# A pooled mix as three products of high and low parts in a decoder layer

## The chip, the core and the metric

The kernel runs on one core of a Trainium2 chip. TensorE multiplies matrices, VectorE and ScalarE do elementwise work and move data out of PSUM, GpSimd (POOL) does some elementwise work too, and SyncE (SP) issues most loads. Each engine takes its instructions strictly in the order in which they were written; where an instruction needs another engine's result it waits on a semaphore, and all behind it on its engine wait too. The metric is the time of one launch on the device, in microseconds (us): the median of three runs.

## The reference

One decoder layer for 256 tokens of width 1024, in float32. The columns of `w_in` give u (512 wide, for the pooling heads) and q, k, v (512 each, for 8 attention heads).

```python
def multiscale_pool(u, w_pool, pool_scale):
    # four groups of 128 channels, windows 2, 4, 8, 16:
    # mean of the trailing window minus the token itself
        groups.append((c_hi - c_lo) / count - uf[..., sl])
    pooled = jnp.stack(groups, axis=2)
    mixed = jnp.einsum('bsgc,gcd->bsgd', pooled, w_pool.astype(jnp.float32))
    return (mixed.reshape(B_, S_, POOL_WIDTH) * pool_scale).astype(u.dtype)

    # the layer
        z = h @ w_in[l]
        pool_out = multiscale_pool(u, w_pool[l], pool_scale[l])
        attn_out = moba_attention(q, k, v).reshape(B_, S_, ATTN_WIDTH)
        mix = jnp.concatenate([pool_out, attn_out], axis=-1) @ w_out[l]
        h = layer_norm(DEEPNORM_ALPHA * h + mix, ln1_g[l], ln1_b[l])
        h = layer_norm(DEEPNORM_ALPHA * h + memory_cross_attention(h, mem, ...), ...)
        h = layer_norm(DEEPNORM_ALPHA * h + swiglu(h, w_gate[l], w_up[l], w_down[l]), ...)
```

With 256 tokens there is one attention block, so the attention is plain causal attention.

## The kernel before

**Products in parts.** Nearly all large products are made of float32 operands that are split in two: a high part, rounded to the type float32r, and a low part, the rest. `split(h, l, ps)` casts on ScalarE (line 483, h) and subtracts on VectorE (line 484, l). `three` (lines 416 to 418) multiplies high by high, high by low and low by high into one accumulator. `proj_both` (lines 431 and 437) has the same three products with the two parts of the activations side by side. A few small products are plain float32: the scores and outputs of the first attention, the transposes, and the four pooled mixes (line 684), which the change touches.

**Weights.** The class `Stream` loads the weights in pieces of 128x1024 (w19, w20, ...), casts each to its high part on ScalarE (line 184, w19h) and subtracts on VectorE (line 191, w19l), some eight pieces ahead of TensorE. A piece that is split frees a raw buffer, and SyncE loads the next piece into it.

**The stretch around the change** (about 50 to 85 us) is written out by hand between the projections of u (`do_u`, accumulators pu) and of the memory's keys (`do_xk`, four chunks of two weight pieces each, accumulators pxk). `run(xk, 8)` lets TensorE do eight steps of that projection, and other work is put between such steps. The four accumulator banks of `accbank` go round: chunk 0 of u, chunk 1 of u, then chunk 0 of the keys (w19, w20) in the banks of the first, chunk 1 (w21, w22) in those of the second. So the first two products with w21h wait until the last two adds of line 704 have read the banks of u's chunk 1.

**The pooling.** u comes out transposed, channels on partitions: a copy on ScalarE (703) and an add on VectorE (704) write it to `upad`. `windows(c)` adds shifted copies on GpSimd (673) for the two groups of a chunk, and scales the first 16 tokens (676). `pool_diff(g)` makes window mean minus token on VectorE (680), in place in `upad`. `mix_pool(g)` multiplies (684); the result, times the scale per channel, is split in cTh (ScalarE, 685) and cTl (VectorE, 686). Groups 0 and 1 belong to chunk 0 of u, groups 2 and 3 to chunk 1. "Mix" one to four below are g = 0 to 3.

`pool_w` holds the four 128x128 mixing matrices and the scales; it is loaded early by one DMA. Activations live in a pool of 11 buffers of 128x2048 floats (tag `a8`), handed out in turn as they come free.

Of the kernel before, what the change touches and what calls it, by code (L numbers as in the profile page):

```python
# [9 lines left out]
F32R = mybir.dt.float32r  # L10
# [4 lines left out]
P = 128  # L15
D = 1024
S = 256
# [9 lines left out]
PADW = 16  # L27
# [14 lines left out]
ALL = slice(None)  # L42
# [4 lines left out]
def r32(t):  # L47
    return t.bitcast(F32)
# [177 lines left out]
def decoder_layer(  # L226
# [3 lines left out]
    nc = tc.nc  # L230
# [3 lines left out]
    ap = ctx.enter_context(tc.tile_pool(name="acts", bufs=A8_BUFS))  # L234
# [10 lines left out]
    def bank(name):  # L245
        return pb.tile([P, 512], F32, tag="b", name=name)
# [59 lines left out]
    class Both:  # L306
# [9 lines left out]
        def pair(self, k, ts=ALL):  # L316
            t, j = self.tiles[k // 4], k % 4
            return t[:, j, 0, ts], t[:, j, 1, ts]
# [29 lines left out]
    pool_w = ep.tile([P, 4 * P + 4], F32, name="pool_w")  # L348
# [59 lines left out]
    upad = ep.tile([P, 4, PADW + S], F32, name="upad")  # L408
# [4 lines left out]
    def three(ps, w, y, start, stop, part=False):  # L413

        (wa, wb), (ya, yb) = w, y
        nc.tensor.matmul(ps, wa, ya, start=start, stop=False, skip_group_check=part)  # L416
        nc.tensor.matmul(ps, wa, yb, start=False, stop=False, skip_group_check=part)  # L417
        nc.tensor.matmul(ps, wb, ya, start=False, stop=stop, skip_group_check=part)  # L418
# [63 lines left out]
    def split(h, l, ps):  # L482
        nc.scalar.copy(h, ps)  # L483
        nc.vector.tensor_sub(l, ps, r32(h))  # L484
# [129 lines left out]
    def scores(hq, t):  # L614
        w = (t + 1) * P
        pss = [bank(f"ps{j}").rearrange("p (h s) -> p h s", h=2) for j in range(2)]
        for h in range(2):
            for j in range(2):
                hs = slice(j * HD, (j + 1) * HD)
                hp = 2 * hq + h  # L620
                nc.tensor.matmul(pss[j][:, h, :w], qT[hs, hp, t * P:(t + 1) * P], kT[hs, hp, :w],
                                 start=True, stop=True)
        todo = []
        for j in range(2):
            pr = sp.tile([P, 2, S], F32, name="pr", bufs=PR_BUFS)[:, :, :w]
            mx = sp.tile([P, 2], F32, name="mx", bufs=6)
            for h in range(2):
                nc.vector.tensor_tensor_reduce(pr[:, h, :], pss[j][:, h, :w], tri[:, S - w:], -1.0, -NEG,  # L628
                                               op0=OP.add, op1=OP.min, accum_out=mx[:, h:h + 1])
            todo.append((pr, exps(pr, pr, mx, -1.0)))  # L630
            probs[hq, t, j] = pr
        for pr, sm in todo:
            scaled(pr, sm)
# [20 lines left out]
    def attend(hp):  # L654
        s0, s1 = pts[hp]
        po = bank("po")
        for j in range(2):
            hs = slice(j * HD, (j + 1) * HD)
            vs = slice((2 * hp + j) * HD, (2 * hp + j + 1) * HD)
            nc.tensor.matmul(po[hs, :S], vt[:, 0, vs], s0[:, j, :], start=True, stop=False)  # L660
            nc.tensor.matmul(po[hs, P:S], vt[:, 1, vs], s1[:, j, :], start=False, stop=True)
        split(cT[0][:, 4 + hp, :], cT[1][:, 4 + hp, :], po[:, :S])
# [4 lines left out]
    def windows(c):  # L667

        cur, n = upad[:, 2 * c:2 * c + 2, :], 1
        for j, g in enumerate((2 * c, 2 * c + 1)):  # L670
# [4 lines left out]
            sums[g] = cur[:, j, :]  # L675
            nc.gpsimd.tensor_mul(sums[g][:, PADW:2 * PADW], sums[g][:, PADW:2 * PADW], fac[:, g, :])

    def pool_diff(g):
        pl = upad[:, g, PADW:]
        nc.vector.scalar_tensor_tensor(pl, sums[g][:, PADW:], 1.0 / WINDOWS[g], pl, op0=OP.mult, op1=OP.subtract)  # L680

    def mix_pool(g):
        pm = bank("pm")
        nc.tensor.matmul(pm[:, :S], pool_w[:, g * P:(g + 1) * P], upad[:, g, PADW:], start=True, stop=True)
        nc.scalar.activation(cT[0][:, g, :], pm[:, :S], AF.Copy, bias=0.0, scale=psc[:, g:g + 1])
        nc.vector.scalar_tensor_tensor(cT[1][:, g, :], pm[:, :S], psc[:, g:g + 1],
                                       r32(cT[0][:, g, :]), op0=OP.mult, op1=OP.subtract)
# [52 lines left out]
    attend(0)  # L740
    scores(1, 1)
    attend(1)
    pool_diff(0)
    pool_diff(1)
    run(u)
    run(xk, 7)
    ws.held = True
    run(xk, 5)
    probs_t(2)
    mix_pool(0)  # L750
    ws.held = False
    run(xk, 8)
    probs_t(3)
    mix_pool(1)
    pool_diff(2)
    run(xk, 8)
    pool_diff(3)
    ws.pace = 2
    run(xk, 8)
    attend(2)  # L760
    attend(3)
    mix_pool(2)
    mix_pool(3)
    run(xk)
# [530 lines left out]
```

## Time and profile before

| | us |
|---|---|
| median of 3 runs (least, most) | 374.09 (374.03, 374.33) |
| the profiled execution | 374.62 |
| its span, first to last instruction | 372.8 |
| TensorE busy (modelled) | 366.7 |
| VectorE busy | 303.1 |
| ScalarE busy | 208.1 |
| GpSimd busy | 24.4 |
| mean granted TensorE clock | 0.999 |

The profiled execution takes 1.8 us more than its span; what lies around the span is the launch. TensorE's busy time is modelled: each product is given a start and an end, and ends overlap the next starts, so the distance of two starts is what a product costs in a row of them. Busy times of VectorE and ScalarE overlap in the same way by about 0.1 us for each instruction.

### The profile page before, as it was taken

What the parts mean: (1) busy time and instruction counts of PE and PEld (TensorE: products, weight loads), DVE (VectorE), ACT (ScalarE), POOL (GpSimd) and SP (SyncE); (2) the same over time, 40 slices, a digit from 0 to 9 for tenths busy, and PEclk for the clock granted to TensorE, in tenths of its full rate; (3) what the DMA queues carried; (4) which work ended last, traced back from release to release, by engine and by line L of the source; (5) the groups of instructions that cost most, each with busy time, mean ns of one, the idle gap of its engine ahead of it and who ended that gap; (6) DMA issues with size and microseconds to landing.
All of it is one profiled execution on the core that took longest, in us unless ns stands there. A gap on an engine that the chain in (4) does not pass through costs nothing.

```text
span 372.8 us, 5508 instructions
## 1 busy us (share of the span) xinstructions
PE 366.7 (98%) x1998; PEld 315.2 (85%) x1998; DVE 303.1 (81%) x493; ACT 208.1 (56%) x336; POOL 24.4 (7%) x31
## 2 busy tenths in 40 slices
PE   9999999999999999999999999999999999999994
PEld 8887878888888889988888888888888888888882
DVE  6878899956699677865889569888888899999994
ACT  5767668635164636644147356766655567774610
POOL 1000033400010000000112000000000000000012
PEclk9999999999999999999999999999999999999999
DMA  7995784658508963688449999955556464896302
GB/s 265 414 416 231 249 310 147 199 173 287 218 2 310 372 220 113 245 289 285 142 65 310 278 303 332 349 180 182 180 194 199 141 225 134 283 355 246 113 0 113
DMA packets 25818, 84.50 MB, mean 227 GB/s; under 512 B 2624, under 2 KB 3392, under 8 KB 25664
## 3 DMA queue, kind: packets, MB, share of 16 engines
q1 hardware_dynamic: 24528, 78.98, 60.2%
q0 software_dynamic: 832, 4.72, 6.4%
q10 hardware_dynamic: 432, 0.46, 0.4%
q8 instruction: 15, 0.25, 0.3%
q14 instruction: 11, 0.09, 0.1%
HBM read 83.10 MB, written 10.49 MB: 251 GB/s over the span
## 4 chain that ended last, share of the span: by engine, by line
PE 98%; ACT 0%; DVE 0%; POOLq 0%; issue 0%
PE pg L431 20%; PE pg L437 10%; PE m L417 5%; PE m L418 5%; PE m L416 5%; PE acc L416 4%; PE acc L417 4%; PE acc L418 4%; PE pxq L431 4%; PE pxk L431 4%; PE pqk L532 4%; PE pqk L535 2%; PE pxk L437 2%; PE pxq L437 2%; PE pu L431 2%; PE xv L416 2%
## 5 line engine op out<-in xcount | busy, mean ns | idle before, releaser
L801 POOL TENSOR_TENSOR rs<-rs,mhalf 128x1 f32<-128x1 f32 x6 | 5.0, 831 | 256.5 <-DVE rs L800 256.5
L483 ACT CAST g<-sg 128x512 fp32r<-128x512 f32 x16 | 9.9, 621 | 21.1 <-DVE sg L1059 13.5
L484 DVE TENSOR_TENSOR g<-sg,g 128x512 fp32r<-128x512 f32 x16 | 11.1, 692 | 11.0 <-ACT g L483 11.0
L1040 DVE TENSOR_TENSOR sg<-pg,sg 128x256 f32<-128x256 f32 x40 | 14.1, 415 | 0.3 <-ACT sg L1039 0.3
L1044 ACT ACTIVATE sg<-sg 128x512 f32<-128x512 f32 x10 | 6.4, 636 | 11.7 <-DVE sg L1040 11.7
L1039 ACT COPY sg<-pg 128x256 f32<-128x256 f32 x40 | 11.8, 376 | 1.3 <-PE pg L437 1.3
L597 ACT ACTIVATE xpr<-xs,mx 128x256 f32<-128x256 f32 x8 | 3.7, 469 | 14.3 <-DVE mx L608 14.3
L597 ACT ACTIVATE pr<-pr,mx 128x128 f32<-128x128 f32 (+1 forms) x16 | 7.1, 445 | 8.0 <-DVE mx L628 8.0
L483 ACT CAST h2T<-tp 128x512 fp32r<-128x512 f32 x4 | 2.3, 586 | 12.9 <-PE tp L494 12.9
L806 DVE SCALAR_TENSOR_TENSOR r<-r,mv,gb 128x512 f32<-128x512 f32 (+2 forms) x12 | 8.2, 721 | 0.0
L793 DVE BATCH_NORM_STATS2 st<-r 128x6 f32<-128x512 f32 (+1 forms) x12 | 8.0, 670 | 0.3
L673 POOL TENSOR_TENSOR win<-upad 128x542 f32<-128x542 f32 x2 | 4.0, 1999 | 55.8 <-DVE upad L704 55.8
L1045 DVE TENSOR_TENSOR sg<-sg 128x512 f32<-128x512 f32 x10 | 6.9, 691 | 0.8
L712 ACT CAST xkTh<-pxk 128x256 fp32r<-128x256 f32 x8 | 2.6, 377 | 8.7 <-PE pxk L437 8.7
L602 DVE RECIPROCAL sm<-sm 128x2 f32<-128x2 f32 x12 | 2.0, 166 | 5.9 <-ACT xpr L597 4.5
L911 PE MATMUL xs<-xkTh,xq 128*128 128x256 f32 x32 | 6.4, 282 | 0.0
L483 ACT CAST h1T<-tp 128x512 fp32r<-128x512 f32 x4 | 2.4, 588 | 7.1 <-PE tp L494 7.1
L714 DVE TENSOR_TENSOR xkl<-pxk,xkTh 128x256 f32<-128x256 f32 x8 | 3.0, 416 | 3.9 <-ACT xkTh L712 3.9
L811 DVE SCALAR_TENSOR_TENSOR h<-r,rs,gb 128x512 f32<-128x512 f32 x8 | 5.7, 747 | 0.1
L673 POOL TENSOR_TENSOR win<-win 128x269 f32<-128x269 f32 (+3 forms) x4 | 5.8, 1446 | 0.2
L184 ACT CAST w39h<-w39r 128x1024 fp32r<-128x1024 f32 x1 | 1.1, 1051 | 7.8 <-PE acc L418 7.8
L911 PEld LDWEIGHTS xs<-xkTh,xq 128*128 128x128 f32 x32 | 5.2, 190 | 0.2
(1137 smaller groups left out, 1291.4 us busy)
## 6 DMA issues: line engine op xcount, KB each, us to landing
sum_z<-in_w_sum SPq DMA_DIRECT2D x2, 1536.0 KB, 10.3
sum_z<-in_w_sum POOLq DMA_DIRECT2D x2, 1536.0 KB, 15.4
gb<-in_ln_g SPq DMA_DIRECT2D x3, 512.0 KB, 6.4
gb<-in_ln_b SPq DMA_DIRECT2D x3, 512.0 KB, 7.4
sum_w<-in_w_sum SPq DMA_DIRECT2D x2, 768.0 KB, 7.2
sum_w<-sum_z POOLq DMA_DIRECT2D x2, 768.0 KB, 10.2
wr<-in_w_qkv SPq DMA_DIRECT2D x5, 256.0 KB, 4.6
mr<-in_mem_t SPq DMA_DIRECT2D x1, 1024.0 KB, 11.4
```

Of the source, the lines that this page charges most:

```text
L416: nc.tensor.matmul(ps, wa, ya, start=start, stop=False, skip_group_check=part)
L417: nc.tensor.matmul(ps, wa, yb, start=False, stop=False, skip_group_check=part)
L418: nc.tensor.matmul(ps, wb, ya, start=False, stop=stop, skip_group_check=part)
L431: nc.tensor.matmul(ps, hi[:, b * P:(b + 1) * P], yT.both(k), start=k == 0, stop=False, skip_group_check=True)
L437: nc.tensor.matmul(ps[:, S:], lo[:, b * P:(b + 1) * P], yT.pair(k)[0], start=False, stop=k == KD - 1, skip_group_check=True)
L483: nc.scalar.copy(h, ps)
L484: nc.vector.tensor_sub(l, ps, r32(h))
L532: nc.tensor.matmul(qk[i], part(i)[0], xT.both(k), start=first, stop=False, skip_group_check=True)
L597: nc.scalar.activation(dst[:, j, :], src[:, j, :], AF.Exp, bias=mx[:, j:j + 1], scale=sign, accum_out=sm[:, j:j + 1])
L911: nc.tensor.matmul(ps[:, t, :], q[:, kk, t * P:(t + 1) * P], k[:, 2 * h + kk], start=n == 0, stop=q is q_lo and kk == 1, skip_group_check= ...
L1039: nc.scalar.copy(y[:, f, :], ps[:, S:])
L1040: nc.vector.tensor_add(y[:, f, :], ps[:, :S], y[:, f, :])
```

## The change

The weights of the four mixes are split once (`split_pool`), into a new tile `pool` of the activation pool. It has two halves, high and low, of 1024 floats each: in each, the first 512 columns are the weights and the two last quarters are for the differences of even and odd groups. Each `pool_diff` now also splits its difference into its quarter. `mix_pool` takes `three` instead of the plain product.

```diff
--- before.py
+++ after.py
@@ -675,13 +675,25 @@
             sums[g] = cur[:, j, :]
             nc.gpsimd.tensor_mul(sums[g][:, PADW:2 * PADW], sums[g][:, PADW:2 * PADW], fac[:, g, :])
 
+    pool_parts = []
+
+    def split_pool():
+        t = ap.tile([P, 2, D], F32R, tag="a8", name="pool")
+        pool_parts.append((t[:, 0], t[:, 1]))
+        split(*pair(pool_parts[0], ALL, slice(0, 4 * P)), pool_w[:, :4 * P])
+
+    def diff_at(g):
+
+        return pair(pool_parts[0], ALL, slice(4 * P + g % 2 * S, 4 * P + (g % 2 + 1) * S))
+
     def pool_diff(g):
         pl = upad[:, g, PADW:]
         nc.vector.scalar_tensor_tensor(pl, sums[g][:, PADW:], 1.0 / WINDOWS[g], pl, op0=OP.mult, op1=OP.subtract)
+        split(*diff_at(g), pl)
 
     def mix_pool(g):
         pm = bank("pm")
-        nc.tensor.matmul(pm[:, :S], pool_w[:, g * P:(g + 1) * P], upad[:, g, PADW:], start=True, stop=True)
+        three(pm[:, :S], pair(pool_parts[0], ALL, slice(g * P, (g + 1) * P)), diff_at(g), True, True)
         nc.scalar.activation(cT[0][:, g, :], pm[:, :S], AF.Copy, bias=0.0, scale=psc[:, g:g + 1])
         nc.vector.scalar_tensor_tensor(cT[1][:, g, :], pm[:, :S], psc[:, g:g + 1],
                                        r32(cT[0][:, g, :]), op0=OP.mult, op1=OP.subtract)
@@ -740,6 +752,7 @@
     attend(0)
     scores(1, 1)
     attend(1)
+    split_pool()
     pool_diff(0)
     pool_diff(1)
     run(u)
```

How the change moves instructions is seen in the order on ScalarE and VectorE. First ScalarE behind the attention of the second pair of heads (cTh<-po), where the pool weights are split; w24 and w25 are weights of the memory's keys, pt a bank of transposes. Before:

```order
L483 CAST cTh<-po 128x256
L184 CAST w24h<-w24r 128x1024
L703 COPY upad<-pu 128x256 x2
L184 CAST w25h<-w25r 128x1024
L649 COPY sb<-pt_794 128x2x128
```

And now:

```order
L483 CAST cTh<-po 128x256
L483 CAST pool<-pool_w 128x512
L483 CAST pool<-upad 128x256 x2
L184 CAST w24h<-w24r 128x1024
L715 COPY upad<-pu 128x256 x2
L184 CAST w25h<-w25r 128x1024
L649 COPY sb<-pt_801 128x2x128
```

Three casts stand ahead of w24h and of the two copies of u that empty its accumulators; the two from upad need VectorE's differences.

VectorE at the same place, before:

```order
L484 TENSOR_TENSOR cTl<-po,cTh 128x256
L680 SCALAR_TENSOR_TENSOR upad<-win,upad 128x256 x2
L191 TENSOR_TENSOR w24l<-w24r,w24h 128x1024
L704 TENSOR_TENSOR upad<-pu,upad 128x256 x2
L191 TENSOR_TENSOR w25l<-w25r,w25h 128x1024
```

And now:

```order
L484 TENSOR_TENSOR cTl<-po,cTh 128x256
L484 TENSOR_TENSOR pool<-pool_w,pool 128x512
L691 SCALAR_TENSOR_TENSOR upad<-win,upad 128x256
L484 TENSOR_TENSOR pool<-upad,pool 128x256
L691 SCALAR_TENSOR_TENSOR upad<-win,upad 128x256
L484 TENSOR_TENSOR pool<-upad,pool 128x256
L191 TENSOR_TENSOR w24l<-w24r,w24h 128x1024
L716 TENSOR_TENSOR upad<-pu,upad 128x256 x2
L191 TENSOR_TENSOR w25l<-w25r,w25h 128x1024
```

Difference and low half take turns, each low half behind a cast of ScalarE, and all of it stands ahead of w24l and of the adds that free the banks of u.

ScalarE again, at the differences of groups 2 and 3, where w28 is a weight of the output projection. Before:

```order
L649 COPY sb<-pt_846 128x2x128
L685 ACTIVATE cTh<-pm,pool_w 128x256
L184 CAST w28h<-w28r 128x1024
L712 CAST xkTh<-pxk 128x256 x2
L184 CAST w29h<-w29r 128x1024
```

And now:

```order
L649 COPY sb<-pt_855 128x2x128
L697 ACTIVATE cTh<-pm,pool_w 128x256
L483 CAST pool<-upad 128x256
L184 CAST w28h<-w28r 128x1024
L483 CAST pool<-upad 128x256
L724 CAST xkTh<-pxk 128x256 x2
L184 CAST w29h<-w29r 128x1024
```

The cast of difference 2 stands ahead of w28h, and that of difference 3 ahead of the keys' casts. On VectorE the low half of difference 2 stands ahead of w28l, and difference 3 with its low half behind it.

## Rows read from the trace of the kernel before

**Rows 1.** The page, sections 1 (busy us, share, instructions) and 4 (chain, by engine).
```profile
PE 366.7 (98%) x1998; PEld 315.2 (85%) x1998; DVE 303.1 (81%) x493; ACT 208.1 (56%) x336; POOL 24.4 (7%) x31
...
PE 98%; ACT 0%; DVE 0%; POOLq 0%; issue 0%
```

**Rows 2.** Timeline, end: start, us, engine, line, operation, tiles, count, [idle before].
```profile
367.55 0.40 ACT L1232 ACTIVATE diag<-ident,rs 128x128 f32<-128x128 f32 x1 [4.13 <-POOL rs L801]
...
368.00 0.91 PE L1235 MATMUL end<-r,diag 128*128 128x384 f32 x2 [1.47 <-ACT diag L1232]
```

**Rows 3.** Timeline of TensorE, 57 to 82 us.
```profile
61.55 0.60 PE L684 MATMUL pm<-upad,pool_w 128*128 128x256 f32 x2
61.80 1.30 PE L437 MATMUL pxk<-mT,w20l 128*128 128x256 f32 x8
62.94 2.01 PE L431 MATMUL pxk<-mT,w21h 128*128 128x512 f32 x8
...
73.05 1.13 PE L684 MATMUL pm<-upad,pool_w 128*128 128x256 f32 x4
73.83 2.19 PE L431 MATMUL pxk<-mT,w24h 128*128 128x512 f32 x8
```

**Rows 4.** Timeline of TensorE, 362 us: products of parts, 128x256.
```profile
362.03 0.28 PE L417 MATMUL m<-w132l,go 128*128 128x256 f32 x1
362.15 0.28 PE L418 MATMUL m<-w132h,go 128*128 128x256 f32 x1
```

**Rows 5.** Timeline of VectorE, 52 to 64 us.
```profile
58.89 0.41 DVE L484 TENSOR_TENSOR cTl<-po,cTh 128x256 fp32r<-128x256 f32 x1
59.23 0.75 DVE L680 SCALAR_TENSOR_TENSOR upad<-win,upad 128x256 f32<-128x256 f32 x2
59.89 1.22 DVE L191 TENSOR_TENSOR w24l<-w24r,w24h 128x1024 fp32r<-128x1024 f32 x1
61.03 0.75 DVE L704 TENSOR_TENSOR upad<-pu,upad 128x256 f32<-128x256 f32 x2
61.70 1.21 DVE L191 TENSOR_TENSOR w25l<-w25r,w25h 128x1024 fp32r<-128x1024 f32 x1
```

**Rows 6.** Timeline of ScalarE, 51 to 60 us.
```profile
58.03 0.35 ACT L483 CAST cTh<-po 128x256 fp32r<-128x256 f32 x1
58.29 1.05 ACT L184 CAST w24h<-w24r 128x1024 fp32r<-128x1024 f32 x1
59.23 0.63 ACT L703 COPY upad<-pu 128x256 f32<-128x256 f32 x2
59.76 1.06 ACT L184 CAST w25h<-w25r 128x1024 fp32r<-128x1024 f32 x1
```

**Rows 7.** The page, section 5: group, count | busy, mean ns | idle, releaser.
```profile
L483 ACT CAST g<-sg 128x512 fp32r<-128x512 f32 x16 | 9.9, 621 | 21.1 <-DVE sg L1059 13.5
L484 DVE TENSOR_TENSOR g<-sg,g 128x512 fp32r<-128x512 f32 x16 | 11.1, 692 | 11.0 <-ACT g L483 11.0
...
L712 ACT CAST xkTh<-pxk 128x256 fp32r<-128x256 f32 x8 | 2.6, 377 | 8.7 <-PE pxk L437 8.7
```

**Rows 8.** Timeline of GpSimd, 60 to 70 us.
```profile
61.86 2.00 POOL L673 TENSOR_TENSOR win<-upad 128x542 f32<-128x542 f32 x1 [5.54 <-DVE upad L704]
...
68.69 0.74 POOL L673 TENSOR_TENSOR win<-win 128x257 f32<-128x257 f32 x1
```

**Rows 9.** Timeline of VectorE, 66 to 80 us.
```profile
68.76 0.95 DVE L680 SCALAR_TENSOR_TENSOR upad<-win,upad 128x256 f32<-128x256 f32 x1 [0.28 <-POOL win L676]
69.63 1.23 DVE L191 TENSOR_TENSOR w28l<-w28r,w28h 128x1024 fp32r<-128x1024 f32 x1
70.79 0.41 DVE L680 SCALAR_TENSOR_TENSOR upad<-win,upad 128x256 f32<-128x256 f32 x1
...
78.25 0.76 DVE L714 TENSOR_TENSOR xkl<-pxk,xkTh 128x256 f32<-128x256 f32 x2 [2.00 <-ACT xkTh L712]
```

**Rows 10.** Windows at the end: length, busy by engine, clock, DMA, GB/s.
```profile
367.00:368.00 1.00, 0.00 (x0) 0.00 (x0) 1.00 (x3) 0.40 (x1) 0.51 (x1) 1.00 0.55 221
```

## The prediction

> **What bounds the kernel now.** I read the page's busy line and its chain of waits first. TensorE is busy for 366.7 of 372.8 us, and the chain that ended last runs through it for 98% [rows 1]. Its only stop worth naming stands at the very end, 1.47 us for the scaled diagonal [rows 2]. So what TensorE loses before that is lost at the end, and no other engine's work costs anything until it makes TensorE wait. Then I read the stretch of the pooled mixes, 58 to 76 us, engine by engine [rows 3, 5, 6, 8, 9]. There TensorE never waits, but VectorE runs without a gap, and TensorE lives on small leads. The lead that matters is this: the last add that empties the accumulators of u (line 704, two adds) starts at 61.03 and ends at 61.78 [rows 5]; the first products of chunk 1 of the memory keys (w21h), which go into the same two banks, start at 62.94 [rows 3]. The second of them starts about 0.23 later (eight take 2.01), so the lead is 63.17 - 61.78 = 1.39 us.
>
> **The products themselves get cheaper.** A plain product of a mix runs as two records. The pair of the first mix starts at 61.55 and its successor at 61.80, and that successor's eight take 1.30 where eight of 128x256 take about 1.12 alone (0.12 apart, with a last one of 0.28, as in rows 4); so the pair costs 0.25 + 0.18 = 0.43. The two pairs of the last mixes cost 73.83 - 73.05 = 0.78, and 0.18 more in the eight behind them (2.19 against 2.01): 0.96 [rows 3]. Products of parts follow each other by 0.12 [rows 4], so three are 0.36. That saves 0.07 in each of the first two mixes and 0.96 - 0.72 = 0.24 in the last two together, 0.38 in all if nothing waits.
>
> **What VectorE and ScalarE get.** Added are one cast and one difference of 128x512, and four casts and four differences of 128x256, with order strict on both engines. The prices: the 128x512 cast 0.62 and difference 0.69, both from SBUF to SBUF, stand in the page; for 128x256 from SBUF there is no row. The cast lies between 0.377 (same size, from PSUM) and 0.62; the difference between 0.41 (same size, one input in PSUM, [rows 5]) and 0.69 [rows 7]. I take 0.38 and 0.41, the same size being nearer than the double. An instruction starts about 0.08 before its predecessor ends on VectorE, 0.10 on ScalarE [rows 5, 6]. A handover I take at 0.05, from 367.55 + 0.40 to 368.00 [rows 2]. The costs do not just add up, because the high half of a difference is cast by ScalarE after VectorE made the difference, and VectorE then waits for that cast before it subtracts.
>
> First place, all in us. ScalarE casts the pool weights at 58.29, where w24h starts now, until 58.91. VectorE subtracts at 59.23, until 59.92. Difference 0: 59.84 to 60.26 (the pair takes 0.75, one 0.42). Its cast: 60.31 to 60.69. Its low half: 60.74 to 61.15. Difference 1: 61.07 to 61.49. Cast: 61.54 to 61.92. Low half until 62.38. Behind that cast stand w24h, 61.82 to 62.87 (1.05), and the copies of u; behind the low half stands w24l, which needs w24h: 62.92 to 64.14 (1.22). So the adds of u start at 64.06 instead of 61.03, shift 3.03, and end at 64.48 and 64.81. The first mix itself is not late: it wants the parts of difference 0 (60.69 and 61.15) and comes at 61.55. But w21h waits until 64.53, and its second product until 64.86 instead of 63.17: 1.69 lost, of which the cheaper first mix gives nothing back, because it lies ahead of the stop. The second mix saves 0.07, so TensorE is 1.62 late when it comes to the third, at 73.05 + 1.62 = 74.67.
>
> Second place. From 61.03 to the difference 2 at 68.76 VectorE has no gap but one of 0.28 for GpSimd's window sum [rows 9], and that sum starts when the adds of u end (61.86 after 61.78, [rows 8]); so both come 3.03 later, difference 2 at 71.79. Now it takes 0.95, where others take 0.41 to 0.42, because it starts 0.07 after a window sum that reads SBUF [rows 8, 9]; that pairing stays. So: difference 2 until 72.74, cast 72.79 to 73.17, low half until 73.63, in time for the third mix. Behind this cast stands w28h, which ScalarE now has done long before: 73.07 to 74.12. VectorE's w28l follows at 74.17, until 75.40 (1.23), difference 3 at 75.32 until 75.73, its cast 75.78 to 76.16, its low half until 76.62. The fourth mix comes at 74.67 + 0.36 = 75.03 and waits for the high half until 76.21 (1.18 lost), then after one product of 0.12 for the low half until 76.67 (0.34). The last two mixes save 0.24.
>
> Sum: 1.69 - 0.07 + 1.18 + 0.34 - 0.24 = 2.90. Against the profiled execution's own 374.62 that is 377.5; the median of the runs shown is 0.53 under it, so 377.0 is forecast.
>
> What I cost at nothing: VectorE and ScalarE are later by some 3 us or more from there on, up to 4.5 at w28l. VectorE waits 2.00 before 78.25 for a cast that waits for TensorE [rows 9], and TensorE itself is 2.9 later there; so no third stop follows. If that cover were gone, each 0.1 of lag beyond it would cost up to 0.1. The parts take a buffer of their own in the activation pool, which moves later tenants to other buffers; the load of the second norm's scale now waits in the queue of SyncE for the last mix, but it stands there behind loads that wait for weights split after the mixes, so that wait is over when its turn comes. The load of the pool weights is not moved.
>
> [...]
>
> **Rivals.**
> Only the first stop. The fourth mix is not late if its parts are there by 75.03. For it: ScalarE is idle when difference 2 comes. Against it: two round trips and w28l stand between, and the sum is 1.2 over. Time: 374.09 + 1.69 - 0.07 - 0.24 = 375.5.
>
> No stop at all. VectorE's own added work ahead of the adds of u is 0.61 + 0.33 + 0.33 = 1.27 without the overlapped ends, and the lead is 1.39. If the round trips cost nothing beside it, the adds come in time, and the cheaper products are all that is left: 374.09 - 0.38 = 373.7. That decides below a shift of 1.34. Against it: the two casts can't start before the differences they read, and w24l can't start before w24h, which stands behind the second cast. Of its chance of 0.11 the larger part stays within what can be told from no change (0.4 is gained at most by these rows).
>
> [...]
> [...]
>
> Longer round trips. If casts and differences cost the upper ends (0.62 and 0.69), the first place gains 4 steps, 2 x 0.24 + 2 x 0.28 = 1.04, the second some 0.8: 378.8.
>
> **How the numbers follow.** Both stops, near the sum: 0.70, from 376.2 to 378.2. Only the first: 0.10, 375.5. No stop: 0.11, 373.7. Longer round trips 0.06, clock 0.03. The range runs from 375.4 to 378.4 and leaves out no stop, the clock and half of the long round trips. A difference under 0.2% (0.75 us) can't be told from none here. Slower by more: 0.70 + 0.10 + 0.06 + 0.03 = 0.89. The 0.11 of no stop is 0.08 within, and 0.03 faster, if the plain products cost more than I read.
>
> **What would show it.** In the profile after: the adds of u start near 64.1; an idle time of TensorE of about 1.7 before w21h, released by VectorE's add; another of about 1.2 before the fourth mix, released by ScalarE's cast, and a short one behind it; w24h cast near 61.8; difference 2 near 71.8 with 0.95; the granted clock 1.00 throughout; mixes of 0.36; from 80 us on the same rows as before, 2.9 later. Wrong would be: adds of u before 62.5, a fourth mix that doesn't wait, or a stop of TensorE after 80 us that isn't there now.

## The result, and the profile after

The changed kernel takes 377.50 us (median of 6 runs, 376.92 to 378.25), the kernel before 374.32 on the same chip (6 runs, 374.03 to 374.89). The ratio is 1.0083, with a 95% interval of 1.0073 to 1.0093: slower by 0.8%. The forecast was 377.0 in a range of 375.4 to 378.4. The profiled execution took 377.73 with a span of 376.0, 3.11 and 3.2 more than before.

The page after: first busy us, share and instructions of each engine, then the chain that ended last, by engine.

```profile
PE 367.2 (98%) x2002; PEld 315.3 (84%) x2002; DVE 305.7 (81%) x498; ACT 209.3 (56%) x341; POOL 23.9 (6%) x31
...
PE 97%; DVE 1%; ACT 1%; issue 0%; POOLq 0%; ACTq 0%
```

TensorE is listed with 0.5 us more than in [rows 1]. That is not more work, for the mixes cost a little less than before (products_only, below): busy time is modelled, and part of a wait between two products of one group counts in it. The eight with w21h take 2.19 instead of 2.01, and the first product of the fourth mix counts for 0.38 where the next could follow after 0.12. So the 3.1 us are waiting, and the chain now runs for 1% through VectorE and for 1% through ScalarE. The longest waits of TensorE (line, what it waited for, us in all, times, longest) say where:

```profile
PE pxk L431 <- DVE upad L716: 1.5, 1, 1.5
PE end L1248 <- ACT diag L1245: 1.5, 1, 1.5
PE pm L416 <- ACT pool L483: 1.0, 1, 1.0
```

The one at the end was there before [rows 2]. The two others are new: the chunk of the memory keys (w21h) behind the adds that empty the banks of u, and the fourth mix behind ScalarE's cast of a difference. Here they stand in the timeline of TensorE after (start, us, engine, line, operation, tiles, count, idle before):

```profile
61.46 0.36 PE L416 MATMUL pm<-pool 128*128 128x256 f32 x1
61.67 0.28 PE L417 MATMUL pm<-pool 128*128 128x256 f32 x1
...
61.90 1.11 PE L437 MATMUL pxk<-mT,w20l 128*128 128x256 f32 x8
64.48 2.19 PE L431 MATMUL pxk<-mT,w21h 128*128 128x512 f32 x8 [1.47 <-DVE upad L716]
...
74.69 0.39 PE L416 MATMUL pm<-pool 128*128 128x256 f32 x1
74.91 0.28 PE L417 MATMUL pm<-pool 128*128 128x256 f32 x1
75.03 0.28 PE L418 MATMUL pm<-pool 128*128 128x256 f32 x1
76.30 0.38 PE L416 MATMUL pm<-pool 128*128 128x256 f32 x1 [0.99 <-ACT pool L483]
76.76 0.39 PE L417 MATMUL pm<-pool 128*128 128x256 f32 x1
76.98 0.28 PE L418 MATMUL pm<-pool 128*128 128x256 f32 x1
77.10 2.00 PE L431 MATMUL pxk<-mT,w24h 128*128 128x512 f32 x8
...
80.85 2.00 PE L431 MATMUL pxk<-mT,w25h 128*128 128x512 f32 x8
```

Against [rows 3], w21h comes 1.54 later (64.48 to 62.94), the third mix 1.64 (74.69 to 73.05), w24h 3.27 (77.10 to 73.83, but its eight then take 2.00 instead of 2.19); w25h stood at 77.77 before and is 3.08 late. From there on nothing is added: the products behind the scaled diagonal start at 371.11, which is 3.11 later than in [rows 2].

The releaser of the first stop is VectorE. Its timeline after, first at the adds of u, then at the last two differences:

```profile
59.79 0.42 DVE L691 SCALAR_TENSOR_TENSOR upad<-win,upad 128x256 f32<-128x256 f32 x1
60.68 0.43 DVE L484 TENSOR_TENSOR pool<-upad,pool 128x256 fp32r<-128x256 f32 x1 [0.47 <-ACT pool L483]
...
61.91 0.42 DVE L484 TENSOR_TENSOR pool<-upad,pool 128x256 fp32r<-128x256 f32 x1 [0.47 <-ACT pool L483]
62.87 1.23 DVE L191 TENSOR_TENSOR w24l<-w24r,w24h 128x1024 fp32r<-128x1024 f32 x1 [0.53 <-ACT w24h L184]
64.01 0.74 DVE L716 TENSOR_TENSOR upad<-pu,upad 128x256 f32<-128x256 f32 x2
...
68.12 2.11 DVE L191 TENSOR_TENSOR w26l<-w26r,w26h 128x1024 fp32r<-128x1024 f32 x1
...
72.31 0.41 DVE L691 SCALAR_TENSOR_TENSOR upad<-win,upad 128x256 f32<-128x256 f32 x1
...
74.19 1.23 DVE L191 TENSOR_TENSOR w28l<-w28r,w28h 128x1024 fp32r<-128x1024 f32 x1 [0.52 <-ACT w28h L184]
75.34 0.42 DVE L691 SCALAR_TENSOR_TENSOR upad<-win,upad 128x256 f32<-128x256 f32 x1
76.28 0.42 DVE L484 TENSOR_TENSOR pool<-upad,pool 128x256 fp32r<-128x256 f32 x1 [0.53 <-ACT pool L483]
```

Three idle times of about 0.5 stand ahead of the adds, each behind a cast of ScalarE, where VectorE had none [rows 5]. The adds start at 64.01, not at 61.03. The other half of each round trip is in ScalarE's timeline after:

```profile
58.25 0.62 ACT L483 CAST pool<-pool_w 128x512 fp32r<-128x512 f32 x1
60.24 0.41 ACT L483 CAST pool<-upad 128x256 fp32r<-128x256 f32 x1 [1.37 <-DVE upad L691]
61.48 0.41 ACT L483 CAST pool<-upad 128x256 fp32r<-128x256 f32 x1 [0.83 <-DVE upad L691]
61.79 1.04 ACT L184 CAST w24h<-w24r 128x1024 fp32r<-128x1024 f32 x1
...
72.81 0.41 ACT L483 CAST pool<-upad 128x256 fp32r<-128x256 f32 x1 [4.61 <-DVE upad L691]
...
75.84 0.40 ACT L483 CAST pool<-upad 128x256 fp32r<-128x256 f32 x1 [1.68 <-DVE upad L691]
```

ScalarE waits too, for VectorE's difference, and w24h, which needs nothing of all this, starts 3.5 us later than in [rows 6] because it is queued behind the casts of the pool's parts.

### The profile page after: what moved, and what is told of

It reads as the page before. It is cut to its first block, busy times and chain, and to the rows that moved or that the text cites. A ratio compares the mean times of both kernels' runs of the same rounds, so it can differ in the third digit from the quotient of the medians.

```text
span 376.0 us, 5525 instructions
## 1 busy us (share of the span) xinstructions
PE 367.2 (98%) x2002; PEld 315.3 (84%) x2002; DVE 305.7 (81%) x498; ACT 209.3 (56%) x341; POOL 23.9 (6%) x31
## 3 DMA queue, kind: packets, MB, share of 16 engines
q0 software_dynamic: 832, 4.72, 6.4%
## 4 chain that ended last, share of the span: by engine, by line
PE 97%; DVE 1%; ACT 1%; issue 0%; POOLq 0%; ACTq 0%
PE pg L431 19%; PE pg L437 10%; PE m L417 5%; PE m L416 5%; PE m L418 5%; PE acc L416 4%; PE acc L417 4%; PE acc L418 4%; PE pxk L431 4%; PE pxq L431 4%; PE pqk L532 4%; PE pqk L535 2%; PE pxq L437 2%; PE pu L431 2%; PE xv L416 2%; PE xv L418 2%
## 5 line engine op out<-in xcount | busy, mean ns | idle before, releaser
L483 ACT CAST pool<-upad 128x256 fp32r<-128x256 f32 x4 | 1.6, 406 | 8.5 <-DVE upad L691 8.5
L484 DVE TENSOR_TENSOR h1T<-tp,h1T 128x512 fp32r<-128x512 f32 x4 | 2.8, 690 | 2.8 <-ACT h1T L483 2.8
L494 PEld LDWEIGHTS tp<-ident,h 128*128 128x128 f32 x32 | 4.0, 140 | 1.0
```

## The experiments

The theory: TensorE loses what the two stops cost, and these come from the order in which ScalarE's and VectorE's instructions stand in their queues (each waits for the other in turn, with work that TensorE needs behind). Rivals: the loss is the amount of work added to VectorE and ScalarE, wherever it stands; or it is in the products of parts themselves. A length tells the loss inside one execution: from the first product of w19h (56.26 before, 56.25 after) to the first of the output projection (83.33, 86.42). It holds all four mixes and both stops. It was 27.07 before and is 30.17 after. Executions start this stretch up to 0.6 us apart, so times of two kernels are compared below as distances inside each. The kernel before ran beside each experiment: its median was 374.45 beside splits_only, late23, diffs_first and all_late, and 374.32 beside the others.

| kernel | median, us | ratio to before | 95% interval | length, us |
|---|---|---|---|---|
| changed | 377.50 | 1.0083 | 1.0073 to 1.0093 | 30.17 |
| splits_only | 376.82 | 1.0064 | 1.0049 to 1.0079 | 29.41 |
| diffs_first | 376.39 | 1.0054 | 1.0040 to 1.0069 | 28.67 |
| high_on_vector | 376.05 | 1.0044 | 1.0027 to 1.0061 | 28.89 |
| late23 | 375.88 | 1.0042 | 1.0026 to 1.0057 | 28.61 |
| diffs_first_both | 374.70 | 1.0006 | 0.9993 to 1.0019 | 27.13 |
| all_late | 374.21 | 0.9993 | 0.9979 to 1.0007 | 26.80 |
| products_only | 374.11 | 0.9984 | 0.9972 to 0.9997 | 26.77 |

**The products alone (products_only).** The kernel before, its mixes as three products of the memory's parts, which are there anyway, so that the mixes compute something else; no split is added.

```diff
-        nc.tensor.matmul(pm[:, :S], pool_w[:, g * P:(g + 1) * P], upad[:, g, PADW:], start=True, stop=True)
+        three(pm[:, :S], mT.pair(g, slice(0, P)), mT.pair(g), True, True)
```

> The kernel before, with three products in each mix on operands that are there already (parts of the memory tokens), so without any split: the mixes compute something else. By the prediction the mixes get cheaper by 0.07, 0.07 and 0.24: 374.0. By what the trace of the changed kernel shows (0.44 from the start of each first mix to its successor, the first of the three taking 0.2 behind plain products) the first two mixes gain nothing: 374.2. If three products were dearer than a plain one (rival), 375 or more.

Its timeline of TensorE, the second mix and the last two:

```profile
65.08 0.27 PE L645 MATMUL pt<-ident,pr 128*128 128x128 f32 x1
65.11 0.36 PE L416 MATMUL pm<-mT 128*128 128x256 f32 x1
...
65.55 1.99 PE L431 MATMUL pxk<-mT,w22h 128*128 128x512 f32 x8
67.38 1.12 PE L437 MATMUL pxk<-mT,w21l 128*128 128x256 f32 x8
...
72.72 0.39 PE L416 MATMUL pm<-mT 128*128 128x256 f32 x1
...
73.54 2.00 PE L431 MATMUL pxk<-mT,w24h 128*128 128x512 f32 x8
```

Measured 374.11, a ratio of 0.9984 (0.9972 to 0.9997): the products cost nothing, they give 0.30 of the length back. From the last transpose ahead of a mix (65.08) to w21l it is 2.30, before 65.33 to 67.70, 2.37: 0.07 saved in the second mix, and 0.07 in the first in the same way (61.28 to 62.70 against 61.45 to 62.94). So the first two mixes do gain; the 374.2 of the expectation took it that they don't. The last two mixes take 72.72 to 73.54, 0.82, and leave the eight behind them at 2.00: against 0.78 + 0.19 before that saves 0.15. The rival of the products falls.

**The splits alone (splits_only).** The changed kernel with the plain product in the mixes; the parts are made and left unused.

```diff
-        three(pm[:, :S], pair(pool_parts[0], ALL, slice(g * P, (g + 1) * P)), diff_at(g), True, True)
+        nc.tensor.matmul(pm[:, :S], pool_w[:, g * P:(g + 1) * P], upad[:, g, PADW:], start=True, stop=True)
```

> The changed kernel with the plain float32 product back in the four mixes; the split parts are made and not used. If the loss comes from the queues of VectorE and ScalarE (theory), the first stop of TensorE stays as it is after the change (w21h starts near 64.5, 1.6 us late), and the fourth mix waits for its difference alone (it ends near 75.8, the mix would come at 75.0): about 0.7 more, together 376.7 against 374.3 before. If the three products cost the time (rival), it falls back to 374.3 to 374.8.

Its timeline of TensorE at both places:

```profile
64.29 2.23 PE L431 MATMUL pxk<-mT,w21h 128*128 128x512 f32 x8 [1.38 <-DVE upad L716]
...
75.63 0.70 PE L696 MATMUL pm<-upad,pool_w 128*128 128x256 f32 x2 [0.31 <-DVE upad L691]
```

376.82, and the length is 2.34 over before. The first stop is there with no product of parts in the kernel. The fourth mix waits only for the difference itself, 0.31, and no longer for its parts. From the third mix to w25h it is 5.30 (74.62 to 79.92), 0.58 over the 4.72 of before, where the changed kernel has 1.44 over. So the first stop is the splits', and most of the second is the mix waiting for them.

**Take one stop away each (late23, diffs_first).** late23 splits the differences 2 and 3 behind the last attention outputs and mixes them there; the first place is as changed. Only the place of the new calls is shown; `pool_diff` no longer splits groups 2 and 3.

```diff
     attend(3)
+    split_diff(2)
+    split_diff(3)
+    run(xk, 14)
     mix_pool(2)
```

> The changed kernel, but the differences of groups 2 and 3 are split only behind the last two attention outputs, and mixes three and four follow 14 steps of the key projection later. By the theory the second stop (1.5 us after the change) is gone and the first stays: 374.3 + 1.6 - 0.2 = 375.7, with no wait of TensorE in any mix. If the amount of added work on VectorE decides and not its place (rival), the time stays at 377.5.

375.88, a length of 28.61: the first stop of 1.47 stays, the second is gone, and the mixes, now between other products of parts, take 0.36 each. diffs_first does the same work as the changed kernel, but at the first place both differences stand ahead of all splits, so that one cast runs beside another's difference. `pool_diff(g, True)` makes the difference without its split.

```diff
+    def pool_first():
+        pool_diff(0, True)
+        pool_diff(1, True)
+        split_pool()
+        for g in range(2):
+            split(*diff_at(g), upad[:, g, PADW:])
...
-    split_pool()
-    pool_diff(0)
-    pool_diff(1)
+    pool_first()
```

> The changed kernel with the same instructions at the first place in another order: both differences first, then the split of the pool weights, then the splits of the two differences, so that VectorE has other work while ScalarE casts. By the theory that the round trips make the shift, the adds of u start near 62.5 instead of 64.0 (shift 1.5 instead of 3.0), the first stop shrinks from 1.6 to about 0.2, the second stays near 1.4: 375.7. If the amount of work makes the shift (rival), the first stop stays at 1.5 or more and the time at 377.3 or more.

VectorE's timeline of diffs_first at that place:

```profile
59.18 0.75 DVE L691 SCALAR_TENSOR_TENSOR upad<-win,upad 128x256 f32<-128x256 f32 x2
59.85 0.68 DVE L484 TENSOR_TENSOR pool<-pool_w,pool 128x512 fp32r<-128x512 f32 x1
60.45 0.75 DVE L484 TENSOR_TENSOR pool<-upad,pool 128x256 fp32r<-128x256 f32 x2
61.35 1.23 DVE L191 TENSOR_TENSOR w24l<-w24r,w24h 128x1024 fp32r<-128x1024 f32 x1 [0.15 <-ACT w24h L184]
62.50 0.75 DVE L724 TENSOR_TENSOR upad<-pu,upad 128x256 f32<-128x256 f32 x2
```

The same instructions end 1.51 earlier, by their order alone: the idle times fall from 0.47, 0.47 and 0.53 to 0.15, and the adds start at 62.50. Half of the shift of 3.0 is gone with the waiting; the other half, 1.5, stays: 1.27 is VectorE's added work (59.85 to the end of the low halves at 61.20, less the usual overlap of 0.08), the rest is the wait for w24h that is left. The listed wait for w21h is gone (it starts at 62.97); the second stop stays, 0.96 of idle time, and its place costs 1.40 (from the third mix to w25h 73.22 to 79.34, against 73.05 to 77.77 before), as much as in the changed kernel (1.44). I expected 375.7 and got 376.39 (375.96 to 376.84), 0.69 more. Of that 0.15 is the kernel before (374.45, where I took 374.3) and 0.20 is in the length, 1.60 over before where I had added up 1.4; the rest, 0.34, is not in the length and stays unexplained. With late23 this run shows that either stop can be taken away without the other.

**Both orders (diffs_first_both).** As diffs_first, and at the second place too the difference 3 stands ahead of both splits (only the second place is shown).

```diff
-    pool_diff(2)
+    pool_diff(2, True)
     run(xk, 8)
-    pool_diff(3)
+    pool_diff(3, True)
+    for g in (2, 3):
+        split(*diff_at(g), upad[:, g, PADW:])
```

> As the run with the differences first, and at the second place too the instructions stand in another order: difference 2, then w28, difference 3, then the splits of both. No work is left out or moved out of the stretch. By the theory the fourth mix's high half is there near 73.2 and its low half near 73.6, when the mix comes (73.7), so that the second stop is gone too, and only the 0.2 at w21h stay: 374.5, no wait of TensorE in any mix. If it is the work and not its order that costs (rival), it stays at 376 or more.

374.70, ratio 1.0006 (0.9993 to 1.0019). Its timeline of TensorE, w21h and the last two mixes:

```profile
60.96 0.27 PE L645 MATMUL pt<-ident,pr 128*128 128x128 f32 x1
...
62.53 2.21 PE L431 MATMUL pxk<-mT,w21h 128*128 128x512 f32 x8
64.58 0.27 PE L643 MATMUL pt<-ident,pr 128*128 128x128 f32 x1
...
72.78 0.39 PE L416 MATMUL pm<-pool 128*128 128x256 f32 x1
...
73.24 0.28 PE L416 MATMUL pm<-pool 128*128 128x256 f32 x1
...
73.59 2.00 PE L431 MATMUL pxk<-mT,w24h 128*128 128x512 f32 x8
```

There is no wait in either mix. This kernel does every instruction of the change (its VectorE is busy for 305.2 us, the changed one's for 305.7, [rows 1] have 303.1), has the same new tile in the activation pool, and is as fast as before. So the amount of work, and the buffers that the tile moved, are not what costs the 3.1.

The splits are not quite free in this order, though. From the last transpose ahead of the first mix (60.96) to the first one behind w21h (64.58) it is 3.62; products_only, with the same products and no splits, has 3.26 (61.28 to 64.54). These 0.36 are in no list of waits. They are lost at w21h, because the 1.5 by which the adds are late, most of it VectorE's added work, is over the lead of 1.39. They are all that this length has over that of products_only (27.13 and 26.77). Against that kernel the splits cost 3.40 in the changed order and 0.36 in this one, and the cheaper products, worth 0.30, cover the 0.36.

**All of it where the engines are idle (all_late).** Splits and mixes stand behind the last attention outputs, between the remaining chunks of the memory keys, and no longer at their former places. Only the new place is shown.

```diff
     attend(3)
+    split_pool()
+    split_diff(0)
+    split_diff(1)
+    run(xk, 12)
+    mix_pool(0)
+    mix_pool(1)
+    split_diff(2)
+    split_diff(3)
+    run(xk, 8)
     mix_pool(2)
```

> The changed kernel with all splits and all four mixes moved behind the last attention outputs, where VectorE and ScalarE have idle time: the same products and the same splits. By the theory no stop of TensorE is left, and the mixes, now between products of the same kind, cost 0.36 each: 374.3 - 0.4 = 373.9. If the added work costs time wherever it stands (rival: more VectorE work or dearer products), it stays over 375.

374.21, ratio 0.9993 (0.9979 to 1.0007), with no stop of TensorE at either place. Its length is 0.27 under before, which the times can't confirm, and 0.03 over that of products_only: here the splits cost next to nothing. No version here is shown to beat the kernel before by a measurable amount while it computes the same.

**No round trip (high_on_vector).** VectorE casts the high parts itself, so that nothing goes to ScalarE and back; the order is the changed kernel's. `split_v` takes the place of `split` in `split_pool` and `pool_diff`.

```diff
+    def split_v(h, l, ps):
+        nc.vector.tensor_copy(h, ps)
+        nc.vector.tensor_sub(l, ps, r32(h))
```

> The changed kernel, but VectorE casts the high parts of the pool's weights and differences itself, so that no split goes through ScalarE. VectorE then has 1.3 us more work ahead of the adds of u, but no handover; each step still waits for the one before it on the same engine. By the theory the adds of u start near 64.0 as after the change (first stop about 1.5), and at the second place w28h is not held up on ScalarE, so the fourth mix waits some 0.7 instead of 1.5: 376.5. If handing over to ScalarE itself were the cost (rival), both stops would shrink to under 0.7: 375 or less.

VectorE's timeline:

```profile
58.74 0.42 DVE L681 CAST pool<-pool_w 128x512 fp32r<-128x512 f32 x1
...
60.25 0.29 DVE L681 CAST pool<-upad 128x256 fp32r<-128x256 f32 x1
...
63.18 0.75 DVE L720 TENSOR_TENSOR upad<-pu,upad 128x256 f32<-128x256 f32 x2
```

376.05 where 376.5 was expected. VectorE's casts were cheaper than I took them, 0.42 and 0.29. The adds come at 63.18 in an execution that is 0.46 ahead of the changed one here (cTl<-po starts at 58.40, not 58.86), so on the same footing they are 0.37 earlier than after the change: the casts take 1.1 of VectorE's time where the three waits took 1.47. w21h still waits for 1.09 (listed behind the add; 1.47 after the change): with VectorE full, its own work in front of the adds delays them too, only less than three waits do. The rival, that handing over to ScalarE is itself the cost, falls by this stop. At the second place the fourth mix is 0.27 late for its high half and 0.34 for its low half (73.87, 74.60, 75.06 on TensorE), some 0.6 where 0.7 was expected; from the third mix to w25h it is 0.54 over before instead of 1.44. There w28h no longer stands behind a cast.

## Why the prediction was right, point by point

**The first stop: right.** The adds were put at 64.06 and came at 64.01; w21h was put at 64.53 and came at 64.48. Each step of that chain is within 0.07: the cast of the weights 58.29 and 58.25, the cast of difference 0 60.31 and 60.24, w24h 61.82 and 61.79, w24l 62.92 and 62.87. Of the prices, the cast of 128x256 was 0.41 where 0.38 was taken; the difference of that size 0.42 to 0.43, near the 0.41. Two casts 0.03 dearer were made up for by handovers of 0.02 to 0.04, where 0.05 was taken. The stop was put at 1.69; the transposes of the second mix's stretch come 1.72 later (66.51 against 64.79). The list of waits has 1.47, because it counts from the modelled end of the product before and leaves out the second product's wait.

**Both mixes ahead of the second place: right.** The second was to save 0.07 and saves 0.08 by the timeline after (66.51 to 69.34 against 64.79 to 67.70). TensorE was to be 1.62 late at the third mix and is 1.64 late. The saving comes otherwise than reckoned: from its first product to the successor the first mix takes 0.44 (61.46 to 61.90), no less than the plain pair, but that product starts 0.02 behind the last transpose, where the plain one started 0.10 behind it.

**The second stop: right.** High half put at 76.21, the fourth mix came at 76.30; low half at 76.67, the second product at 76.76. Both are 0.09 late, from a cast that costs 0.02 more and from handovers of 0.06 to 0.08 where 0.05 was taken (difference 3 ends at 75.76, its cast starts at 75.84 and ends at 76.24). Without a wait the fourth mix would have started at 75.15 (75.03 and one product of 0.12). The stops measure 76.30 - 75.15 = 1.15 and 76.76 - 76.30 - 0.12 = 0.34, where 1.18 and 0.34 stood. The list has 0.99 for the first, again from a modelled end.

**The mis-sized term: "the last two mixes save 0.24".** They save 0.05. Three products were taken at 0.36; they take that only behind other products of parts, as in late23. In the changed kernel both take 0.46 without the waits: the third mix has 0.22 between its first two products (74.69, 74.91), the fourth 0.22 between the last two (76.76, 76.98). products_only puts the first of these at 0.10 (0.15 saved, not 0.24); the second is there only where the mix has waited. The sign "mixes of 0.36" failed with it. So the sum is 1.72 - 0.08 + 1.15 + 0.34 - 0.05 = 3.08, which is the lateness of w25h, against 2.90. On 374.62 that gives 377.70; the profiled execution took 377.73. Of the 0.50 between the forecast of 377.0 and the median of 377.50, 0.23 is the kernel before, whose median was 374.09 of three runs then and 374.32 of six beside the change, and 0.18 is the sum; the rest is within the spread of the runs.

**A step that failed without effect: "that pairing stays".** Difference 2 was put at 71.79 with 0.95. It starts at 72.31, behind the last sum (which ends at 72.00), takes 0.41, and yet ends at 72.72, where 72.74 was put. GpSimd's second and third window sum and VectorE's w26l, before:

```profile
63.94 4.49 POOL L673 TENSOR_TENSOR win<-win 128x538 f32<-128x538 f32 x2
65.14 1.21 DVE L191 TENSOR_TENSOR w26l<-w26r,w26h 128x1024 fp32r<-128x1024 f32 x1
```

GpSimd's timeline after:

```profile
66.91 2.24 POOL L673 TENSOR_TENSOR win<-win 128x538 f32<-128x538 f32 x2
```

Two sums took 4.49 before, and difference 2 waited 0.28 for GpSimd and then took 0.95 beside another sum [rows 8, 9]. Now they take 2.24, and it is VectorE's w26l that takes 2.11 instead of 1.21. On VectorE the two splits of w26 and w27 take 0.93 more; less the wait of 0.28 and the overlap of 0.08 that a wait takes away, and less the 0.54 of difference 2, that makes 0.03. That these cancel is luck: the 72.74 was right for a reason that did not hold. In both traces the one that takes longer ends about where it would if it ran behind what it overlaps: after, that is 70.36 for w26l (the third sum starts at 68.07 and takes 1.08, w26l takes 1.21 before), and w26l ends at 70.23; before, that is 68.58 for the third sum behind w27l (67.50 and 1.08), and it ends at 68.43. Which of the two is the longer one does not follow from the starts: the third sum is 0.04 to 0.05 ahead of w26l in both traces, and before it was the sum that took longer (3.33), after it was w26l. So difference 2 lost its 0.95, but the time did not vanish: it moved to another instruction.

**The rivals.** Only the first stop, 375.5: this is late23, which measures 375.88, so the price was good and the case did not happen. No stop, 373.7: products_only, 374.11, and nearly diffs_first_both, 374.70; the gain of 0.38 was really 0.30 of length. That rival's condition, a shift below 1.34, is not met even in diffs_first, where most of the waiting is gone: the shift is 1.5 there. The clock: it didn't fall, which the stretch holding the first stop shows (windows of after; length, busy us of TensorE, its weight loads, VectorE, ScalarE, GpSimd, then the granted clock, DMA share, GB/s):

```profile
58.00:78.00 20.00, 17.47 (x110) 14.54 (x109) 16.79 (x33) 11.50 (x25) 7.15 (x6) 1.00 0.38 128
63.00:64.40 1.40, 0.01 (x1) 0.00 (x0) 1.40 (x3) 1.40 (x4) 0.00 (x0) 1.00 0.00 0
```

TensorE does next to nothing for 1.4 us there and its granted clock stays at 1.00; what [rows 10] showed for a stop at the end holds in the middle. Neither trace shows a clock below 1.00 at a stop between two products, so the prediction's 0.03 for it has no run behind it. Longer round trips: not by prices, as above. And no third stop: the lag that VectorE and ScalarE had at 76 us was taken up by their idle time, as forecast; the last stretch is shifted by 3.11 as a whole.

## What to carry over

Where two engines work in order and take turns at one value (difference, cast, low half), each turn of a difference cost a wait on both here (0.47 and 0.47 on VectorE, 1.37 and 0.83 on ScalarE, at the first place), and what stood behind in either queue was late by it, related or not (w24h by 3.5); with all first steps ahead of the second ones the same instructions cost 0.36 us of length here instead of 3.40 (medians 374.70 and 377.50). Count the lead of the most urgent instruction *behind* the new ones (here 1.39 us at the adds of u) and not the busy share of the engine. The work itself counts against that lead too: 1.27 us of it ahead of the adds used up nearly all of the 1.39. Behind the last attention outputs, where VectorE and ScalarE have idle time (single waits of 2.00 and 3.15 in the kernel before), the same work cost nothing that could be measured (all_late).

## What the runs showed of the hardware that was not expected

- Products of parts, 128x256, followed each other at 0.12, but the first behind plain float32 products was followed after 0.20 to 0.22 (61.46 to 61.67, 74.69 to 74.91), and in a mix that had to wait the last two were 0.22 apart as well. In the first two mixes this cost nothing, since the first product followed the last transpose after 0.02 instead of 0.10; in the third and fourth it cost 0.10 each. The records do not say what takes the 0.10.
- VectorE cast from SBUF to SBUF faster than ScalarE did: 0.42 against 0.62 for 128x512, 0.29 against 0.41 for 128x256, while its difference of 128x512 took 0.69 (high_on_vector, and ScalarE after). From 256 to 512 columns VectorE's cast grew by 0.13 and its difference by 0.27 (0.42 to 0.69).
- Whether GpSimd's window sum or VectorE's split takes longer when they overlap changed from kernel to kernel: w26l took 2.11 after and in four of the seven others, w27l 2.09 and 2.10 in all_late and high_on_vector, and in products_only, as before, w26l and w27l took 1.21 to 1.22 and difference 2 took 0.95. What decides it stays open; it was not tried.
